# Sums of weight blocks: VectorE subtractions replaced by adding transfers from memory to memory

## The chip, the cores and the metric

The kernel runs on one core of one Trainium2 chip. The metric is the time of one execution on the device in microseconds (us), lower is better. The engines are named as in the profile: PE is TensorE (matmuls), with PEld for its weight loads; DVE is VectorE; ACT is ScalarE; POOL is GpSimd; SP is SyncE, which here issues nearly all transfers. A trailing q (SPq, POOLq) means the engine's instruction queue.

## The reference

A decoder trunk of two layers on 1024 tokens of width 1024, all float32. Layer one mixes tokens with HGRN2, a gated linear recurrence of 8 heads; layer two with sliding-window attention. Each layer ends with a gated feed-forward part:

```python
def conv_ffn(h, w_in, conv_w, conv_b, w_out):
    u = h @ w_in                                   # (1024, 1024) @ (1024, 5632)
    u = causal depthwise convolution of width 3 over u, + conv_b
    a, b = jnp.split(u, 2, axis=-1)
    return (jax.nn.silu(a) * b) @ w_out            # (1024, 2816) @ (2816, 1024)
...
    for layer in range(DEPTH):
        mix = hgrn2_mixer(...) if layer < N_A_LAYERS else swa_sink_mixer(...)
        h = layer_norm(ALPHA * h + mix, ...)
        h = layer_norm(ALPHA * h + conv_ffn(h, ...), ...)
```

The change is about the last product, the down-projection by `w_out`, and about the HGRN2 mixer of layer one, during which its weights are prepared.

## The kernel before, in words

Every float32 matrix is split into a high and a low part, and a product is three TensorE matmuls (`mm3`, lines 169 to 171). TensorE's order is written out in the program: a small planner (`Order`, `od`) hands out pieces of slower work (the recurrence's steps) between the matmuls of the projections. In the HGRN2 stage SyncE's order is the program's too; the orders on VectorE, ScalarE and GpSimd are made by the scheduler when the kernel is built, from its own estimate of when each operand is ready, with the program's order as priority. `tc.issue_after(x)` keeps what is made inside it behind `x` on `x`'s engine.

**The down-projection.** `Down` computes it in Winograd's form of Strassen's method: the activations (as blocks A) and the weights (as blocks B) are cut into 2 x 2 blocks, and seven block products take the place of eight. Some products need sums of weight blocks. There are four, s1 = B12 - B11, s3 = B22 - B12, s2 = B22 - s1, s4 = B21 - s2, all in the DRAM tensor `bsd` (one for each layer). `Down.sum_b` (line 539) loads pieces of 128 x 512 from it, `operands` makes the differences of activation blocks, and `evacuate` (line 589) adds each finished product to the rows of `Y` that it belongs to, in each of four pairs of token blocks.

**Where the sums are made.** No weight sum depends on the activations, so all are made early, in the HGRN2 stage. This stage is cut into 60 slots: 4 for the first head, then 8 for each of 7 heads (four half projections for q and f, four blocks for i and g). `slot_begin` (line 988) and `slot_end` (line 1007) stand around each. A table fixes for each of 22 pieces in which slot its two rows of blocks are loaded into rows of `Y` (line 998), in which VectorE makes the four subtractions (line 1005) and in which the result is stored to `bsd` (line 993). The subtractions are queued in `pending`; `between`, called in the recurrence, places two or four of them behind an instruction of the recurrence, and `slot_end` places the rest.

**The recurrence.** `recur` runs one head behind the projections. Its steps go through levels; in `update` (line 844) VectorE multiplies `qp` (line 851) and GpSimd `kp` (line 853), and the score matmuls of the next level (line 175) read both. GpSimd also makes small norms (lines 943 and 944). Weights of the projections of the next head are loaded by `load` (line 139, on SyncE) into three buffers `raw`, and split by ScalarE (line 151) and VectorE (line 144).

Of the kernel before, what the change touches and what calls it, by code (L numbers as in the profile page):

```python
# [10 lines left out]
F32 = mybir.dt.float32  # L11
# [76 lines left out]
def trunk(ctx: ExitStack, tc: tile.TileContext, a: dict, out: bass.AP):  # L88
    nc = tc.nc
# [8 lines left out]
    drp = ctx.enter_context(tc.tile_pool(name="drp", bufs=1, space=bass.MemoryType.DRAM))  # L98
# [11 lines left out]
    ynd = drp.tile([P, 8, D], F32, name="ynd")  # L110
    gd = drp.tile([P, NF, S], F32, name="gd")
    rbd = drp.tile([16, P, 2 * P], F32, name="rbd")
    bsd = [drp.tile([P, FF // 256, 2, D], F32, name=f"bsd{l}") for l in range(2)]

    def psmm():
        return mmp.tile([P, 512], F32, name="psmm")
# [400 lines left out]
    class Down:  # L517
# [19 lines left out]
            nc.sync.dma_start(dst, self.w[f0:f0 + P, bc * 512:(bc + 1) * 512])  # L537

        def sum_b(self, dst, k, t):
            i, j = {1: (0, 0), 3: (0, 1), 4: (1, 0), 2: (1, 1)}[t]  # L540
            nc.sync.dma_start(dst, self.sums[:, k, i, j * 512:(j + 1) * 512])

        def operands(self, i, k):
            p = self.ORDER[i]
            R = self.R[:, :, k, :] if i > 1 else None
            x = self.raw[0].rearrange("p (b n) -> p b n", b=2)
            self.raw = self.raw[1:] + self.raw[:1]
            if p == 1:
                self.block_a(x[:, 0], k, 0, 0)
                self.block_b(x[:, 1], k, 0, 0)  # L550
            elif p == 2:
                self.block_a(x[:, 0], k, 0, 1)
                self.block_b(x[:, 1], k, 1, 0)
            elif p == 5:
                self.block_a(R[:, 0], k, 1, 0)
                self.block_a(x[:, 0], k, 1, 1)
                self.sum_b(R[:, 1], k, 1)
                tt(R[:, 0], R[:, 0], x[:, 0], op=add)
                x = R
            elif p == 6:  # L560
                self.block_a(x[:, 0], k, 0, 0)
                self.sum_b(R[:, 1], k, 2)
                tt(R[:, 0], R[:, 0], x[:, 0], op=sub)
                x = R
            elif p == 7:
                self.block_a(x[:, 0], k, 1, 1)
                self.sum_b(x[:, 1], k, 3)
                tt(x[:, 0], x[:, 0], R[:, 0], op=sub)
            elif p == 3:
                self.block_a(x[:, 0], k, 0, 1)  # L570
                self.block_b(x[:, 1], k, 1, 1)
                tt(x[:, 0], x[:, 0], R[:, 0], op=sub)
            else:
                self.block_a(x[:, 0], k, 1, 1)
                self.sum_b(x[:, 1], k, 4)
            slots = {3: [10, 11, 12, 13, 14, 2, 7, 8, 9, 0, 1], 4: [6, 3, 4, 5, 2, 0, 1, 6, 3, 4, 5]}
            j = slots[p][k] if p in slots and not self.last else (i * self.H + k) % 15
            j = (j + 4) % 7 if j < 7 else j
            if j < 6:
                hl = hl_at(j)  # L580
            elif j == 6:
                hl = tail["R"][:, :2, :]
            else:
                hl = T[:, (j - 7) // 4, (j - 7) % 4 * 2:(j - 7) % 4 * 2 + 2, :]
            hl = hl.rearrange("p h (b n) -> p h b n", b=2)
            split(hl[:, 0], hl[:, 1], x)
            return hl

        def evacuate(self, p, tb, ps, ln):
            lo, hi = [Y[:, t, :].rearrange("p (h n) -> p h n", h=2) for t in (tb, tb + 4)]  # L590
            both = ps.unsqueeze(1).to_broadcast([P, 2, 512])
            if p == 1:
                for y in (lo, hi):
                    nc.vector.scalar_tensor_tensor(y, y, ALPHA, both, op0=ALU.mult, op1=ALU.add)
            elif p in (6, 7):
                tt(hi, hi, both, op=add)
            for y in {2: [lo[:, 0]], 5: [lo[:, 1], hi[:, 1]], 6: [lo[:, 1]], 3: [lo[:, 1]], 4: [hi[:, 0]]}.get(p, []):
                tt(y, y, ps, op=add)

            if p in (2, 3, 4, 7):  # L600
                ln_half(tb if p in (2, 3) else tb + 4, 0 if p in (2, 4) else 1)
            if p in (3, 4):
                task = ln(tb if p == 3 else tb + 4, self)
                if task is not None:
                    self.tasks.append(od.spawn(task))
# [53 lines left out]
    x = a["x"][0]  # L659
# [3 lines left out]
    with tc.tile_pool(name="t", bufs=1, reuse_waits="tile") as raws, hgrn_pool as hp:  # L663
# [154 lines left out]
        def recur(h, qs, fg, kp):  # L818
# [25 lines left out]
            def update(i):  # L844
                m = 1 << i
                nb = S // (2 * m)
                Tm, off = level
                qv = qp.rearrange("p (b u m) -> p b u m", u=2, m=m)
                kv = kp.rearrange("p (b u m) -> p b u m", u=2, m=m)
                tv = Tm[:, off:off + 2 * nb].rearrange("p (b u) -> p b u", u=2)  # L850
                nc.vector.tensor_tensor(qv[:, :, 1, :], qv[:, :, 1, :],
                                        tv[:, :, 0:1].to_broadcast([P, nb, m]), op=ALU.mult)
                (nc.gpsimd if i else nc.vector).tensor_tensor(kv[:, :, 0, :], kv[:, :, 0, :],  # L853
                                        tv[:, :, 1:2].to_broadcast([P, nb, m]), op=ALU.mult)
                noff = 0 if i == 0 else off + 2 * nb
                last = nc.vector.tensor_tensor(tot[:, noff:noff + nb], tv[:, :, 0], tv[:, :, 1], op=ALU.mult)
                level[:] = tot, noff
                return last

            yield 0.0  # L860
            r0 = hp.tile([P, S], F32, name="St")
# [23 lines left out]
            for i in range(2, 7):  # L885
# [3 lines left out]
                else:  # L889
# [9 lines left out]
                    def put():  # L899
                        for b in range(P // (2 * m)):  # L900
                            o = 2 * m * b
                            nc.scalar.copy(A[o:o + m, :, o + m:o + 2 * m], pv[o:o + m, :, o + m:o + 2 * m])
                last = update(i)
                between(put() or last, 2)
                if i == 4:
                    for b in range(P // BL):
                        bs = slice(b * BL, (b + 1) * BL)
# [35 lines left out]
            nc.gpsimd.tensor_scalar(ss, ss, 1.0 / P, RMS_EPS, op0=ALU.mult, op1=ALU.add)  # L943
            nc.gpsimd.tensor_tensor(ss, ss, nhalf.to_broadcast([P, NB]), op=ALU.pow)
            nc.vector.tensor_tensor(og, pv, G, op=ALU.mult)
            between(nc.vector.tensor_tensor(og, og, ss.unsqueeze(2).to_broadcast([P, NB, P]), op=ALU.mult), 4)
            values_done[0] = h
            yield 8.0
            ps = psax()
# [10 lines left out]

        pairs = FF // 256
        lead = [0, 3, 2, 2, 2, 2, 1, 1]
        begins = [4] + [8 * h + lead[h] for h in range(1, NH)]
        busy = {s for c in begins for s in (c - 1, c)}
        free, loads, sums, stores = {r: 0 for r in (0, 2, 4, 6)}, {}, {}, {}
        for i in range(2 * pairs):
            for s in range(8 * NH):
                for r in free:  # L970
                    at = next(n for n in range(s + 2, 9 * NH) if n not in busy and n not in sums)
                    if s not in loads and free[r] <= s and at + 1 <= begins[r] + 4:
                        break
                else:
                    continue
                break
            loads[s], sums[at], stores[at + 1], free[r] = (i, r), (i, r), (i, r), at + 2
        slot_no = [-1]
        anchor, pending = {}, []

        def between(inst, n):

            with tc.issue_after(inst.ins):
                while pending and n:
                    pending.pop(0)()
                    n -= 1

        def slot_begin():
            slot_no[0] += 1
            n = slot_no[0]  # L990
            if n in stores:
                i, r = stores[n]
                nc.sync.dma_start(bsd[i // pairs][:, i % pairs, :, :], Y[:, r:r + 2, :])
            if n in loads:
                i, r = loads[n]
                for k in range(2):
                    row = (k * pairs + i % pairs) * P
                    nc.sync.dma_start(Y[:, r + k, :], a["ffn_w_out"][i // pairs][row:row + P, :])
            if n in sums:
                r = sums[n][1]  # L1000
                blocks = Y[:, r:r + 2, :].rearrange("p a (b n) -> p a b n", b=2)
                (b11, b12), (b21, b22) = [(blocks[:, k, 0], blocks[:, k, 1]) for k in range(2)]

                for x, y, z in ((b11, b12, b11), (b12, b22, b12), (b22, b22, b11), (b21, b21, b22)):
                    pending.append(lambda x=x, y=y, z=z: tt(x, y, z, op=sub))

        def slot_end(act, dve, *makes):
            anchor["act"], anchor["dve"] = act, dve or anchor.get("dve", act)
            with tc.issue_after(anchor["act"].ins), tc.issue_after(anchor["dve"].ins):
                for make in makes:  # L1010
                    make()
                while pending:
                    pending.pop(0)()

        values_done = [-1]
        wo = a["hgrn_w_out"][0]
# [393 lines left out]
```

## Time and profile before

| | |
|---|---|
| times of three runs | 2218.33, 2218.30, 2216.71 us, median 2218.3 |
| the profiled execution, span from first to last instruction | 2212.6 us |
| mean granted TensorE clock | 0.998 |
| busy: PE, DVE, ACT, POOL | 2177.4, 1787.0, 931.6, 177.7 us |
| moved by DMA | 281.16 MB, mean 127 GB/s |

For the profiled execution the profile gives the span alone; what lies around it (launch and end) is seen only as the distance to the times of the runs. In a row of the profile, `out<-in` are tiles of the program, `x88` is the number of instructions, and "idle before" is the time in which the engine stood still just before them, with what ended it. A matmul's recorded end is modelled, and successive matmuls overlap in the records.

### The profile page before, as it was taken

What the parts mean: (1) busy time and instruction counts of PE and PEld (TensorE: products, weight loads), DVE (VectorE), ACT (ScalarE), POOL (GpSimd) and SP (SyncE); (2) the same over time, 40 slices, a digit from 0 to 9 for tenths busy, and PEclk for the clock granted to TensorE, in tenths of its full rate; (3) what the DMA queues carried; (4) which work ended last, traced back from release to release, by engine and by line L of the source; (5) the groups of instructions that cost most, each with busy time, mean ns of one, the idle gap of its engine ahead of it and who ended that gap; (6) DMA issues with size and microseconds to landing.
All of it is one profiled execution on the core that took longest, in us unless ns stands there. A gap on an engine that the chain in (4) does not pass through costs nothing.

```text
span 2212.6 us, 33398 instructions
## 1 busy us (share of the span) xinstructions
PE 2177.4 (98%) x13135; PEld 1812.6 (82%) x13135; DVE 1787.0 (81%) x2415; ACT 931.6 (42%) x1601; POOL 177.7 (8%) x196
## 2 busy tenths in 40 slices
PE   8999999999999999999999999999999999999998
PEld 7888888888888888887888887778888888887887
DVE  2777666566789888888997788887899888889987
ACT  4333333332844443344334446655554443343431
POOL 0121111210100000000000012211000000000001
PEclk9999999999999999999999999999999999999999
DMA  5555443252222222238854431114123222249663
GB/s 196 191 191 172 153 172 116 69 125 86 87 85 86 84 78 86 86 96 272 279 171 130 115 89 34 34 63 138 67 96 96 78 75 85 86 144 318 202 215 134
DMA packets 231943, 281.16 MB, mean 127 GB/s; under 512 B 29977, under 2 KB 160746, under 8 KB 228970
## 3 DMA queue, kind: packets, MB, share of 16 engines
q1 hardware_dynamic: 228736, 276.53, 38.5%
q10 hardware_dynamic: 3050, 2.49, 0.9%
q8 instruction: 103, 1.69, 0.3%
q14 instruction: 54, 0.44, 0.1%
HBM read 213.96 MB, written 65.01 MB: 126 GB/s over the span
## 4 chain that ended last, share of the span: by engine, by line
PE 82%; DVE 9%; DMA 3%; ACT 3%; issue 2%; POOL 1%; SPq 0%; ACTq 0%; DVEq 0%; POOLq 0%
PE psmm L169 17%; PE psmm L171 16%; PE psmm L170 16%; PE psax L171 8%; PE psax L169 8%; PE psax L170 8%; PE psax L175 3%; DVE T L144 1%; PE psmm L175 1%; DMA rx<-in_ffn_w_in_dram 1%; DVE HL L144 1%; PE psax L179 1%; ACT Y L244 1%; PE psax L1200 1%; PE psax L1203 1%
## 5 line engine op out<-in xcount | busy, mean ns | idle before, releaser
L169 PE MATMUL psmm<-T,HL 128*128 128x512 f32 x768 | 308.1, 401 | 0.0
L170 PE MATMUL psmm<-T,HL 128*128 128x512 f32 x768 | 300.7, 392 | 3.8 <-DVE T L144 2.1
L171 PE MATMUL psmm<-T,HL 128*128 128x512 f32 x768 | 301.3, 392 | 0.0
L474 DVE SCALAR_TENSOR_TENSOR Y<-Y,cwt 128x1023 f32<-128x1023 f32 (+1 forms) x176 | 225.3, 1280 | 40.1 <-ACT Y L472 39.9
L472 ACT ACTIVATE Y<-Y,cwt 128x1024 f32<-128x1024 f32 x88 | 109.1, 1240 | 263.6 <-DVE Y L461 260.0
L169 PE MATMUL psmm<-HL,T 128*128 128x256 f32 (+1 forms) x656 | 199.6, 304 | 1.5 <-ACT T L196 1.5
L171 PE MATMUL psmm<-HL,T 128*128 128x256 f32 (+1 forms) x656 | 195.4, 298 | 1.6 <-DVE T L144 1.6
L170 PE MATMUL psmm<-HL,T 128*128 128x256 f32 (+1 forms) x656 | 195.1, 297 | 1.2 <-DVE HL L144 1.2
L196 ACT CAST HL<-rx 128x1024 fp32r<-128x1024 f32 (+1 forms) x137 | 140.3, 1045 | 122.6 <-DMA rx<-in_ffn_w_in_dram 33.3
L144 DVE TENSOR_TENSOR HL<-rx,HL 128x1024 fp32r<-128x1024 f32 (+1 forms) x137 | 165.9, 1213 | 14.9 <-ACT HL L196 14.3
L171 PEld LDWEIGHTS psmm<-T,HL 128*128 128x128 f32 x768 | 144.6, 188 | 33.5 <-issue 1.9
L170 PEld LDWEIGHTS psmm<-T,HL 128*128 128x128 f32 x768 | 144.7, 188 | 31.3 <-DVE T L144 2.9
L169 PEld LDWEIGHTS psmm<-T,HL 128*128 128x128 f32 x768 | 144.6, 188 | 31.3 <-issue 1.4
L171 PE MATMUL psax<-T,HL 128*128 128x512 f32 x352 | 137.6, 391 | 0.0
L169 PE MATMUL psax<-T,HL 128*128 128x512 f32 x352 | 137.5, 391 | 0.0
L170 PE MATMUL psax<-T,HL 128*128 128x512 f32 x352 | 137.4, 390 | 0.0
L169 PEld LDWEIGHTS psmm<-HL,T 128*128 128x128 f32 x656 | 126.2, 192 | 8.1 <-issue 2.5
L171 PEld LDWEIGHTS psmm<-HL,T 128*128 128x128 f32 x656 | 126.0, 192 | 5.7 <-DVE T L144 2.5
L170 PEld LDWEIGHTS psmm<-HL,T 128*128 128x128 f32 x656 | 126.2, 192 | 4.9 <-DVE HL L144 1.7
L218 POOL TENSOR_TENSOR rs<-rs,nhalf 128x1 f32<-128x1 f32 x32 | 26.0, 813 | 1291.4 <-DVE rs L217 1291.1
L853 POOL TENSOR_TENSOR kp<-kp,tot 128x512 f32<-128x512 f32 x48 | 72.9, 1519 | 290.0 <-PE psax L175 149.3
L144 DVE TENSOR_TENSOR HL<-raw,HL 128x1024 fp32r<-128x1024 f32 x51 | 64.0, 1254 | 21.7 <-ACT HL L151 21.6
(295 smaller groups left out, 5257.9 us busy)
## 6 DMA issues: line engine op xcount, KB each, us to landing
rx<-in_ffn_w_in_dram SPq DMA_DIRECT2D x136, 256.0 KB, 3.4
rx<-gd SPq DMA_DIRECT2D x118, 256.0 KB, 3.7
Y<-in_ffn_w_out_dram SPq DMA_DIRECT2D x44, 512.0 KB, 6.0
bsd<-Y SPq DMA_DIRECT2D x22, 1024.0 KB, 4.8
gd<-Y SPq DMA_DIRECT2D x44, 512.0 KB, 2.7
rx<-in_ffn_w_out_dram SPq DMA_DIRECT2D x54, 256.0 KB, 4.0
R<-bsd SPq DMA_DIRECT2D x44, 256.0 KB, 4.3
Y<-in_ffn_w_in_dram SPq DMA_DIRECT2D x40, 256.0 KB, 3.3
```

Of the source, the lines that this page charges most:

```text
L144: make = lambda e: e.tensor_tensor(lo, src, hi.bitcast(F32), op=ALU.subtract)
L169: nc.tensor.matmul(ps, st(0), mv(0), start=start, stop=False)
L170: nc.tensor.matmul(ps, st(0), mv(1), start=False, stop=False)
L171: nc.tensor.matmul(ps, st(1), mv(0), start=False, stop=stop)
L175: nc.tensor.matmul(ps, lhsT, rhs, start=start, stop=stop, **kw)
L179: nc.tensor.transpose(ps, src, ident)
L196: nc.scalar.copy(hi, src)
L218: nc.gpsimd.tensor_tensor(rs, rs, nhalf, op=ALU.pow)
L244: nc.scalar.activation(hf[:, kc, :], ps[:, k * P:(k + 1) * P], AF.Identity, bias=shift, scale=scale)
L472: nc.scalar.activation(c, u, AF.Identity, bias=cwt[:, l, 3, ci:ci + 1], scale=cwt[:, l, 2, ci:ci + 1])
L474: nc.vector.scalar_tensor_tensor(c[:, sh:], u[:, :S - sh], cwt[:, l, 2 - sh, ci:ci + 1], c[:, sh:], op0=ALU.mult, op1=ALU.add)
L853: (nc.gpsimd if i else nc.vector).tensor_tensor(kv[:, :, 0, :], kv[:, :, 0, :], tv[:, :, 1:2].to_broadcast([P, nb, m]), op=ALU.mult)
```

## The change

The sums are no longer made on VectorE. Each layer's four sums become four DRAM tensors of 1408 x 512, in which 8 parts in all (2 layers, 4 parts of 352 rows) are filled by transfers from memory to memory: SyncE copies a block (`nc.sync.dma_start`), and a transfer issued from GpSimd with `accum_op=add` adds another block to it. Since a transfer can only add, all sums are now sums without a minus: s1 = B12 + B11, s3 = B12 + B22, s2 = s1 + B22, s4 = s2 + B21. The operand differences and the evacuations get other signs to fit. A part takes six slots in six stages, and a new part starts every seven slots: copies of stage 0, 2 and 4 are issued at a slot's beginning, additions of stage 1, 3 and 5 at a slot's end. `between` and its calls in `recur` go.

```diff
-    bsd = [drp.tile([P, FF // 256, 2, D], F32, name=f"bsd{l}") for l in range(2)]
+    bsd = [[drp.tile([FF // 2, D // 2], F32, name=f"bs{l}{t}") for t in range(4)] for l in range(2)]
...
-            i, j = {1: (0, 0), 3: (0, 1), 4: (1, 0), 2: (1, 1)}[t]
-            nc.sync.dma_start(dst, self.sums[:, k, i, j * 512:(j + 1) * 512])
+            nc.sync.dma_start(dst, self.sums[t - 1][k * P:(k + 1) * P, :])
...
-                tt(R[:, 0], R[:, 0], x[:, 0], op=add)
+                tt(R[:, 0], x[:, 0], R[:, 0], op=sub)
...
+            left, right = [Y[:, tb::4, h * 512:(h + 1) * 512] for h in range(2)]
             lo, hi = [Y[:, t, :].rearrange("p (h n) -> p h n", h=2) for t in (tb, tb + 4)]
             both = ps.unsqueeze(1).to_broadcast([P, 2, 512])
             if p == 1:
-                for y in (lo, hi):
-                    nc.vector.scalar_tensor_tensor(y, y, ALPHA, both, op0=ALU.mult, op1=ALU.add)
-            elif p in (6, 7):
-                tt(hi, hi, both, op=add)
-            for y in {2: [lo[:, 0]], 5: [lo[:, 1], hi[:, 1]], 6: [lo[:, 1]], 3: [lo[:, 1]], 4: [hi[:, 0]]}.get(p, []):
-                tt(y, y, ps, op=add)
+                for y, op in ((left, add), (right, sub)):
+                    nc.vector.scalar_tensor_tensor(y, y, ALPHA, both, op0=ALU.mult, op1=op)
+            elif p == 5:
+                tt(right, right, both, op=sub)
+            elif p == 6:
+                tt(right, right, both, op=add)
+                tt(hi[:, 0], hi[:, 0], ps, op=sub)
+            elif p == 7:
+                tt(hi[:, 0], hi[:, 0], ps, op=add)
+                tt(hi[:, 1], hi[:, 1], ps, op=sub)
+            else:
+                y, op = {2: (lo[:, 0], add), 3: (lo[:, 1], sub), 4: (hi[:, 0], add)}[p]
+                tt(y, y, ps, op=op)
...
-                last = update(i)
-                between(put() or last, 2)
+                update(i)
+                put()
...
+        NCH, RCH = 4, FF // 8
+        plan = {}
+        for i in range(2 * NCH):
+            for stage in range(6):
+                plan.setdefault(2 + 7 * i + stage, []).append((i // NCH, i % NCH, stage))
+        slot_no, anchor = [-1], {}
+
+        def sum_step(l, c, stage):
+
+            b1, b2, b3, b4 = [bsd[l][t][c * RCH:(c + 1) * RCH, :] for t in range(4)]
+            blk = lambda i, j: a["ffn_w_out"][l][i * FF // 2 + c * RCH:i * FF // 2 + (c + 1) * RCH,
+                                                 j * D // 2:(j + 1) * D // 2]
+            copies = {0: ((b1, blk(0, 1)), (b3, blk(0, 1))), 2: ((b2, b1),), 4: ((b4, b2),)}
+            sums = {1: ((b1, blk(0, 0)), (b3, blk(1, 1))), 3: ((b2, blk(1, 1)),), 5: ((b4, blk(1, 0)),)}
+            for dst, src in copies.get(stage, ()):
+                nc.sync.dma_start(dst, src)
+            for dst, src in sums.get(stage, ()):
+                nc.gpsimd.dma_start(dst, src, accum_op=ALU.add)
 
         def slot_begin():
             slot_no[0] += 1
-            n = slot_no[0]
...
+            for step in plan.get(slot_no[0], ()):
+                if step[2] % 2 == 0:
+                    sum_step(*step)
 
         def slot_end(act, dve, *makes):
             anchor["act"], anchor["dve"] = act, dve or anchor.get("dve", act)
             with tc.issue_after(anchor["act"].ins), tc.issue_after(anchor["dve"].ins):
+                for step in plan.get(slot_no[0], ()):
+                    if step[2] % 2:
+                        sum_step(*step)
                 for make in makes:
                     make()
-                while pending:
-                    pending.pop(0)()
```

More of the change, by code (lines that the diff above doesn't have):

```diff
@@ L562, in operands @@
                 self.sum_b(R[:, 1], k, 2)
-                tt(R[:, 0], R[:, 0], x[:, 0], op=sub)
+                tt(R[:, 0], R[:, 0], x[:, 0], op=add)
                 x = R
@@ L567, in operands @@
                 self.sum_b(x[:, 1], k, 3)
-                tt(x[:, 0], x[:, 0], R[:, 0], op=sub)
+                tt(x[:, 0], R[:, 0], x[:, 0], op=sub)
             elif p == 3:
@@ L571, in operands @@
                 self.block_b(x[:, 1], k, 1, 1)
-                tt(x[:, 0], x[:, 0], R[:, 0], op=sub)
+                tt(x[:, 0], R[:, 0], x[:, 0], op=sub)
             else:
@@ L855, in update @@
                 noff = 0 if i == 0 else off + 2 * nb
-                last = nc.vector.tensor_tensor(tot[:, noff:noff + nb], tv[:, :, 0], tv[:, :, 1], op=ALU.mult)
+                nc.vector.tensor_tensor(tot[:, noff:noff + nb], tv[:, :, 0], tv[:, :, 1], op=ALU.mult)
                 level[:] = tot, noff
-                return last
             yield 0.0
@@ L945, in recur @@
             nc.vector.tensor_tensor(og, pv, G, op=ALU.mult)
-            between(nc.vector.tensor_tensor(og, og, ss.unsqueeze(2).to_broadcast([P, NB, P]), op=ALU.mult), 4)
+            nc.vector.tensor_tensor(og, og, ss.unsqueeze(2).to_broadcast([P, NB, P]), op=ALU.mult)
             values_done[0] = h
@@ L957, in recur @@
                     split_scaled(T[:, 0, h, ts], T[:, 1, h, ts], ps[:, ts], par[:, 80:81])
-        pairs = FF // 256
         lead = [0, 3, 2, 2, 2, 2, 1, 1]
[L965 to L984, printed above, removed]
-                    pending.pop(0)()
-                    n -= 1
+        NCH, RCH = 4, FF // 8
[14 more added lines that the diff above has]
+                nc.gpsimd.dma_start(dst, src, accum_op=ALU.add)
@@ L988, in slot_begin @@
         def slot_begin():
             slot_no[0] += 1
-            n = slot_no[0]
[L991 to L1005, printed above, removed]
+            for step in plan.get(slot_no[0], ()):
+                if step[2] % 2 == 0:
+                    sum_step(*step)
@@ L1009, in slot_end @@
             with tc.issue_after(anchor["act"].ins), tc.issue_after(anchor["dve"].ins):
+                for step in plan.get(slot_no[0], ()):
+                    if step[2] % 2:
+                        sum_step(*step)
                 for make in makes:
                     make()
-                while pending:
-                    pending.pop(0)()
         values_done = [-1]
```

## The prediction

> **What bounds the kernel now.** I read the page first (busy shares and chain), then the busy time in stretches of 100 us, then who TensorE waited for in the stage that the change touches, then the rows of the pieces themselves.
>
> ```profile
> span 2212.6 us, 33398 instructions
> PE 2177.4 (98%) x13135; PEld 1812.6 (82%) x13135; DVE 1787.0 (81%) x2415; ACT 931.6 (42%) x1601; POOL 177.7 (8%) x196
> PE 82%; DVE 9%; DMA 3%; ACT 3%; issue 2%; POOL 1%; SPq 0%; ACTq 0%; DVEq 0%; POOLq 0%
> ```
>
> TensorE is busy 98% of the span and carries 82% of the chain; VectorE is the only other engine with a share there that counts. The sums of weight blocks run in the first mixer (HGRN2), at 55.6 to 417.4 us by their row further down. In the stretches there (PE, PEld, DVE, ACT, POOL, clock, DMA share, GB/s) it reads:
>
> ```profile
> 100.00:200.00 100.00, 99.69 (x1166) 88.77 (x1166) 73.98 (x118) 30.88 (x81) 21.49 (x16) 1.00 0.58 199
> 200.00:300.00 100.00, 100.00 (x1011) 90.88 (x1010) 67.89 (x108) 32.48 (x79) 15.51 (x12) 1.00 0.49 168
> 300.00:400.00 100.00, 98.31 (x1044) 86.78 (x1043) 63.14 (x97) 34.19 (x84) 18.90 (x16) 1.00 0.33 111
> 400.00:500.00 100.00, 95.87 (x1109) 83.72 (x1108) 57.17 (x84) 35.08 (x71) 19.49 (x14) 0.98 0.45 107
> ```
>
> TensorE has 0.3 + 0 + 1.7 + 4.1 = 6.1 us of idle time in these 400 us, while VectorE is busy 57 to 74% and GpSimd under 22%. TensorE's waits from 50 to 520 us (total, times, longest) are:
>
> ```profile
> PE psmm L780 <- DVE og L945: 2.0, 1, 2.0
> PE psmm L170 <- issue: 1.7, 1, 1.7
> PE psax L175 <- DVE qp L851: 1.4, 3, 0.5
> PE psmm L170 <- DVE HL L144: 1.2, 2, 0.6
> PE psax L175 <- DVE og L869: 0.9, 1, 0.9
> ```
>
> So the stage is bound by TensorE, whose order is written out by hand and is not changed. Work taken off VectorE can be worth only what is left in that list; anything that makes TensorE late costs in full.
>
> **The change part by part.** *VectorE's 88 subtractions go.* Their rows, by form and by source line (there: shortest, median, longest in ns, first and last start):
>
> ```profile
> L1005 DVE TENSOR_TENSOR Y<-Y 128x512 f32<-128x512 f32 x88 | 70.0, 796 | 4.2 <-DMA Y<-in_ffn_w_out_dram 3.0
> L1005 DVE TENSOR_TENSOR Y<-Y x88: 675/692/1605, 55.6 to 417.4; 128x512 f32<-128x512 f32 x88
> ```
>
> That is 70.0 us of VectorE. On the path lie only the waits for the recurrence's operands, L851 with 1.4 and L869 with 0.9 us: a gain of 2.3, of which I take 2. The wait at L780 lies in one place, after an activation chain; L144's are splits that remain. The bounds of this gain are 0 and the 6.1 us of all idle time, of which 4.1 lie after 400 us, where the subtractions end at 417.4.
>
> *SyncE's transfers change.* Out go 44 loads of 512 KB and 22 stores of 1 MB; in come 32 copies from memory to memory of 352 rows x 2 KB = 704 KB (8 parts, 4 copies each). Rows: KB, then median us from issue to landing; then the issue times and what SyncE waited for.
>
> ```profile
> Y<-in_ffn_w_out_dram SPq DMA_DIRECT2D x44, 512.0 KB, 6.0
> bsd<-Y SPq DMA_DIRECT2D x22, 1024.0 KB, 4.8
> L993 SPq DMA_DIRECT2D bsd<-Y x22: 326/338/4132, 59.5 to 419.0; - x22
> SPq L993 <- DVE Y L1005: 240.6, 18, 40.0
> SPq L998 <- DMA bsd<-Y: 40.3, 13, 4.5
> ```
>
> Issuing is about 0.34 us each, so 66 x 0.34 = 22 us against 32 x 0.34 = 11 us on a queue that is mostly waiting: nothing on the path. By the load's pace (6.0 us for 512 KB) a copy of 704 KB lands after 8.3 us, by the store's (4.8 us for 1 MB) after 3.3 us. What matters is the waiting in order: the copy of block sum 1 into 2 waits until the addition into 1 has landed, that of 2 into 4 until the addition into 2 has, and the loads of the next head's projection weights are queued behind them. Before, the same queue stood 240.6 us for VectorE's sums, 13.4 us each and 40.0 at most. How much the weights bear is seen where SyncE issues them and where ScalarE first uses them:
>
> ```profile
> 227.25 6.06 SPq L139 DMA_DIRECT2D raw<-in_hgrn_w_in_dram  x4
> 257.61 3.74 SPq L139 DMA_DIRECT2D raw<-in_hgrn_w_in_dram  x2
> 258.64 1.04 ACT L151 CAST HL<-raw 128x1024 fp32r<-128x1024 f32 x1
> 287.88 1.05 ACT L151 CAST HL<-raw 128x1024 fp32r<-128x1024 f32 x1
> raw<-in_hgrn_w_in_dram SPq DMA_DIRECT2D x16, 512.0 KB, 8.3
> ```
>
> The group issued by 233.3 has landed by 241.6 at 8.3 us and is used at 258.6: 17 us of cover. The next, issued by 261.4 and landed by 269.7, is used at 287.9: 18 us. I cost SyncE's new waits at nothing, hidden by these 17 us; if that cover is gone, every further microsecond is TensorE's (the second rival).
>
> *GpSimd issues 32 adding transfers of 704 KB.* No DMA on GpSimd is in the trace. Its issue I bound by SyncE's 0.34 us below and its longest, 4.1 us, above; I take 1.5 us, GpSimd's ordinary instruction. Each also waits, in GpSimd's order, until the copy that it adds to has landed. Queued behind it are the recurrence's updates (kp, L853) and the small norms (L943, L944). The updates of one head, the first of the next, and the score matmuls that wait for them:
>
> ```profile
> 182.89 1.61 POOL L853 TENSOR_TENSOR kp<-kp,tot 128x512 f32<-128x512 f32 x1 [9.42 <-PE psax L175]
> 186.29 1.11 POOL L853 TENSOR_TENSOR kp<-kp,tot 128x512 f32<-128x512 f32 x1 [1.79 <-PE psax L175]
> 189.93 1.52 POOL L853 TENSOR_TENSOR kp<-kp,tot 128x512 f32<-128x512 f32 x1 [2.54 <-PE psax L175]
> ...
> 197.49 1.49 POOL L853 TENSOR_TENSOR kp<-kp,tot 128x512 f32<-128x512 f32 x1 [2.39 <-PE psax L175]
> ...
> 240.72 1.60 POOL L853 TENSOR_TENSOR kp<-kp,tot 128x512 f32<-128x512 f32 x1 [12.04 <-PE psax L175]
> 185.38 0.76 PE L175 MATMUL psax<-qp,kp 128*32 128x32 f32 x64
> 189.02 0.76 PE L175 MATMUL psax<-qp,kp 128*32 128x32 f32 x64
> 192.67 0.70 PE L175 MATMUL psax<-qp,kp 128*32 128x32 f32 x32
> ```
>
> An update ends at 184.50, 187.40, 191.45 and is used at 185.38, 189.02, 192.67: slack 0.9, 1.6, 1.2, mean 1.2 us. The updates come every 3.6 us from 182.89 to 198.98, 16.1 us of a head's 57.8 (182.89 to 240.72): 28% of the time. Eight slots a head make a slot 7.2 us. A hold of w us in the series delays an update by w - 1.8 on average (half the pitch), and TensorE by w - 1.8 - 1.2. With the issue alone, w = 1.5, that is nothing. The additions come in 8 x 3 = 24 groups, so 24 x 28% = 6.7 meet the series. For the hold, 0 is the lower end (the addition is placed a slot behind its copy and finds it landed). The upper one is 10 us: a copy at the load's pace, 8.3 us, and 1.5 of issue. I take 5 us, near the longest wait that SyncE had for a landing (4.5 us). Then 6.7 x (5 - 3.0) = 13.4, with those that begin just ahead of the series 14 us. With 10 us it is 24 x (28% + 9%) = 8.9 meetings of 7 us, 62 us.
>
> The Trainium skill's page "DMA: Bandwidth & Descriptors" (Anatomy of one DMA) fits a GpSimd-issued transfer as about 2.0 us plus its bytes at 436 GB/s. For 704 KB that makes an estimated 3.7 us; the trace's 512 KB load, 6.0 us where the fit gives 3.2, does not agree. With copies so quick the hold would shrink to some 2 us and the sum to a gain of 2: the first rival.
>
> *The signs of the seven products.* Rows of the evacuations before:
>
> ```profile
> L596 DVE TENSOR_TENSOR Y<-Y,psax 128x1024 f32<-128x1024 f32 x4 | 4.9, 1216 | 0.0
> L598 DVE TENSOR_TENSOR Y<-Y,psax 128x512 f32<-128x512 f32 x12 | 8.0, 683 | 1.1 <-PE psax L171 1.1
> ```
>
> Product 5 has one instruction of 1024 columns in place of two of 512 (2 x 683 - 1216 = 150 ns saved, 4 token blocks, 2 layers), product 7 the reverse: nil. The operand differences swap inputs in place: nil. Reading the sums back takes the same 256 KB a piece, off TensorE's path: nil.
>
> The sum: 2212.6 - 2 + 14 = 2224.6 us of span. The runs' median, 2218.3, lies 5.7 us above the profiled span, launch and end outside the instructions; with it 2230.
>
> **The rivals.** *Nothing is held.* The additions find their copies landed and GpSimd, idle 78% and more, hides the issue; what is left is the gain: 2216, and at best, with all idle time of the stage gone, 2218.3 - 6.1 = 2212.2. For it: the 1.2 us of slack and the slot between copy and addition. Against: GpSimd's order is set when the kernel is built, and there a transfer is only a guess of its landing. To be faster by over 0.2% (4.4 us, about what a measurement of this kernel can tell from no change) it needs most of the 6.1 us, though the waits named for VectorE's operands are 2.3: little chance.
>
> *SyncE's order paces the stage.* One chain per part: copies 1 and 3, both additions, copy 2, its addition, copy 4, and only then the next part, which comes every 7 slots, 50.6 us. With copies of 8.3 us and additions of twice that (they read the target too), SyncE is held 8.3 + 16.6 + 8.3 + 16.6 = 50 us where each pair runs side by side, and 16.6 + 33.2 + 8.3 + 16.6 = 75 us where it runs one behind the other. The surplus over 50.6 is paid in each of 8 parts: nothing at 50, 93 us halfway (62), 195 at 75. It decides from an addition of 8.6 us (pairs one behind the other: 24.9 + 3 x 8.6 = 50.6) to one of 17 us (side by side: 16.6 + 2 x 17). For it: SyncE's order is fixed, and L998 already waits for a landing 13 times. Against: at the store's pace, 3.3 us a copy and 6.6 an addition, the chain is 20 to 33 us, and the weights have 17 us of cover.
>
> The Trainium skill, on the page "DMA: Bandwidth & Descriptors" (Two DMAs through the same engine are not ordered), wants the issuing engine to wait for the first transfer's semaphore before a dependent one; by it both holds are real waits of SyncE and GpSimd. The trace agrees: SyncE's L998 waits for the landing of bsd, 40.3 us in 13 times.
>
> **How the numbers follow.** Held updates, 48%: 2223 to 2280, likeliest 2230. Nothing held, 35%: 2212 to 2222, of this 10% below 2213.9. SyncE paces, 17%: from 2223 up, most of it over 2280 (2311 halfway). Faster by over 0.2% is 0.10, within 0.2% is 0.25, slower 0.65. The range goes from 2212 (all idle time gone) to 2280 (holds of 10 us) and leaves out some 15 in 100.
>
> **What would show it.** Right: no L1005 on VectorE (70 us less); in GpSimd's waits, adding transfers that wait for a copy, several us each; TensorE's list from 50 to 520 us gains waits on POOL kp L853 of 10 to 20 us in all, and the stage ends that much later. The first rival: no such waits. The second: TensorE or ScalarE wait for DMA raw<-in_hgrn_w_in, and SyncE's longest waits are for additions over 14 us. I would be wrong altogether if time moved after 520 us, where only signs change.

## The result, and the profile after

The changed kernel is slower by 6%: 2349.76 us median (2345.98 to 2355.46, 4 runs) against 2218.32 (2216.71 to 2220.05, 4 runs) on the same chip, a ratio of 1.0597 with a 95% interval of 1.0583 to 1.0611. The forecast was 2230 us in a range of 2212 to 2280: the sign is right, the size is out by more than a factor of ten (131 us more instead of 12).

The page of the changed kernel: span; busy time by engine; TensorE's granted clock in 40 slices of 59 us; the chain by engine.

```profile
span 2351.2 us, 33300 instructions
PE 2210.4 (94%) x13135; PEld 1840.7 (78%) x13135; DVE 1713.4 (73%) x2327; ACT 930.0 (40%) x1601; POOL 206.3 (9%) x228
PEclk9897988989999999999999999999999999999999
PE 73%; DMA 8%; DVE 7%; issue 5%; ACT 3%; POOL 2%; SPq 0%; ACTq 0%; DVEq 0%; POOLq 0%
```

VectorE lost 73.6 us (1787.0 to 1713.4), and the span grew by 138.6 us all the same (the runs' medians differ by 131: the profiled executions are single ones). Of the 138.6, TensorE's idle time is 105.6 (2351.2 - 2210.4 = 140.8, against 35.2 before), and 33.0 are the same 13135 matmuls taking longer (2177.4 to 2210.4). The clock row says where: it has digits under 9 in the first nine slices only (a digit is the clock in tenths).

Busy time in stretches (us, PE, PEld, DVE, ACT, POOL, clock, DMA share, GB/s), the mixer first, then one stretch of the up-projection:

```profile
100.00:200.00 100.00, 86.14 (x824) 78.07 (x825) 42.14 (x73) 26.27 (x70) 21.93 (x19) 0.89 0.48 107
200.00:300.00 100.00, 76.72 (x812) 68.79 (x810) 33.55 (x57) 22.38 (x53) 17.21 (x15) 0.88 0.52 120
300.00:400.00 100.00, 71.80 (x774) 63.11 (x775) 29.20 (x50) 19.81 (x48) 20.45 (x17) 0.86 0.51 107
400.00:500.00 100.00, 86.02 (x812) 75.08 (x811) 36.05 (x65) 29.42 (x73) 18.27 (x15) 0.90 0.45 109
...
900.00:1000.00 100.00, 100.00 (x438) 81.81 (x437) 88.43 (x101) 42.38 (x50) 0.00 (x0) 1.00 0.25 79
```

Where 1011 to 1166 matmuls ran in 100 us before, 774 to 824 run now, with TensorE idle 14 to 28% and its clock at 0.86 to 0.90. From the up-projection on nothing is changed (438 matmuls in the last row, 437 in the same 100 us before). Who TensorE waited for up to 700 us (total, times, longest):

```profile
PE psax L175 <- POOL kp L860: 74.2, 10, 16.3
PE psax L179 <- DVE og L952: 26.9, 4, 9.5
...
PE psax L179 <- POOL kp L860: 4.3, 1, 4.3
```

These 15 waits sum to 105.4 us, which is all of the new idle time (105.6). Eleven are for GpSimd's update of kp (L860; L853 before). Four are for og on VectorE (L952), which takes its factor from the norms that GpSimd works out in ss (L949 and L950; L943 and L944 before). No weight load of the recurrence is in this list. What GpSimd itself waited for at the additions (L987):

```profile
POOL bs L987 <- DMA bs<-bs: 130.8, 12, 25.7
POOL bs L987 <- issue: 109.0, 14, 10.5
...
POOL bs L987 <- DMA bs<-in_ffn_w_out_dram: 72.6, 6, 21.7
```

GpSimd stood still ahead of each of the 32 additions, 312.4 us in all and 9.8 us on average; such a stand is called a hold. Two kinds are to be told apart: 18 holds (203.4 us) end with the landing of the copy that is added to, and 14 (109.0 us) have no releaser in the trace ("issue"). One head's stretch of GpSimd's timeline, with TensorE's matmul that waited (start, us, engine, line, idle before):

```profile
211.95 1.05 POOL L987 DMA_DIRECT2D bs<-in_ffn_w_out_dram  x1 [11.45 <-DMA bs<-bs]
220.84 0.95 POOL L987 DMA_DIRECT2D bs<-in_ffn_w_out_dram  x1 [7.85 <-issue]
228.22 0.94 POOL L987 DMA_DIRECT2D bs<-in_ffn_w_out_dram  x1 [6.43 <-issue]
228.84 1.50 POOL L860 TENSOR_TENSOR kp<-kp,tot 128x512 f32<-128x512 f32 x1
230.39 1.08 PE L175 MATMUL psax<-qp,kp 128*32 128x32 f32 x64 [16.26 <-POOL kp L860]
```

Three additions stand in GpSimd's order directly ahead of the update. The second is issued 7.9 us after the first has been, the third 6.4 us after the second; only then may the update run, and TensorE has lost 16.26 us. Additions issue in 0.95 us and land a median of 7.7 us later (issues of the transfers: KB, us to landing):

```profile
bs<-in_ffn_w_out_dram POOLq DMA_DIRECT2D x32, 704.0 KB, 7.7
...
bs<-in_ffn_w_out_dram SPq DMA_DIRECT2D x16, 704.0 KB, 7.8
bs<-bs SPq DMA_DIRECT2D x16, 704.0 KB, 5.7
```

So the second addition starts about when the first has landed, and the third when the second has: as if GpSimd had room for one such transfer at a time. The other kind of hold is seen a head later, in the timeline of SyncE and GpSimd together:

```profile
209.01 41.50 SPq L139 DMA_DIRECT2D raw<-in_hgrn_w_in_dram  x2
250.56 0.58 SPq L985 DMA_DIRECT2D bs<-bs  x1
256.91 0.96 POOL L987 DMA_DIRECT2D bs<-in_ffn_w_out_dram  x1 [10.93 <-DMA bs<-bs]
```

GpSimd stands from 245.98 for a copy that SyncE issues only at 250.56, because the copy is behind two loads of projection weights, the second of which is issued at 250.1; the copy then lands after some 6 us. The loads themselves wait until VectorE has split the weights loaded before (L144). SyncE's longest waits, up to 700 us, are these, 365.6 us where the kernel before has 56.8:

```profile
SPq L139 <- DVE HL L144: 365.6, 18, 40.7
```

The instructions of the copies and of the additions, by source line (shortest, median, longest in ns, first and last start):

```profile
L985 SPq DMA_DIRECT2D bs<-in_ffn_w_out_dram x16: 505/603/2038, 22.6 to 490.8; - x16
L985 SPq DMA_DIRECT2D bs<-bs x16: 474/481/582, 59.0 to 545.2; - x16
```

```profile
L987 POOL DMA_DIRECT2D bs<-in_ffn_w_out_dram x32: 932/954/1213, 31.5 to 550.4; - x32
```

With the start of each of these 32 and 32 from the timelines, 100 of the 203 us in the 18 holds pass before the copy is issued. In about 25 of these the copy itself waits for the addition issued just before (four holds); in 75, SyncE is still at something else. The remaining 104 us are copies in flight.

### The profile page after: what moved, and what is told of

It reads as the page before. It is cut to its first block, busy times and chain, and to the rows that moved or that the text cites. A ratio compares the mean times of both kernels' runs of the same rounds, so it can differ in the third digit from the quotient of the medians.

```text
span 2351.2 us, 33300 instructions
## 1 busy us (share of the span) xinstructions
PE 2210.4 (94%) x13135; PEld 1840.7 (78%) x13135; DVE 1713.4 (73%) x2327; ACT 930.0 (40%) x1601; POOL 206.3 (9%) x228
## 4 chain that ended last, share of the span: by engine, by line
PE 73%; DMA 8%; DVE 7%; issue 5%; ACT 3%; POOL 2%; SPq 0%; ACTq 0%; DVEq 0%; POOLq 0%
PE psmm L169 14%; PE psmm L171 14%; PE psmm L170 14%; PE psax L171 8%; PE psax L170 8%; PE psax L169 8%; DMA bs<-in_ffn_w_out_dram 4%; DMA bs<-bs 2%; PE psax L175 2%; DVE HL L144 1%; PE psmm L175 1%; PE psax L179 1%; DVE T L144 1%; ACT Y L244 1%; PE psax L1189 1%
## 5 line engine op out<-in xcount | busy, mean ns | idle before, releaser
L169 PE MATMUL psmm<-T,HL 128*128 128x512 f32 x768 | 314.0, 409 | 0.0
L170 PE MATMUL psmm<-T,HL 128*128 128x512 f32 x768 | 305.4, 398 | 2.1 <-DVE T L144 2.1
L171 PE MATMUL psmm<-T,HL 128*128 128x512 f32 x768 | 305.7, 398 | 0.0
L472 ACT ACTIVATE Y<-Y,cwt 128x1024 f32<-128x1024 f32 x88 | 109.0, 1238 | 264.2 <-DVE Y L461 260.6
L169 PE MATMUL psmm<-HL,T 128*128 128x256 f32 (+1 forms) x656 | 204.5, 312 | 1.8 <-ACT T L196 1.8
L171 PE MATMUL psmm<-HL,T 128*128 128x256 f32 (+1 forms) x656 | 199.3, 304 | 2.1 <-DVE T L144 2.1
L170 PE MATMUL psmm<-HL,T 128*128 128x256 f32 (+1 forms) x656 | 199.3, 304 | 1.2 <-DVE HL L144 1.2
L144 DVE TENSOR_TENSOR HL<-rx,HL 128x1024 fp32r<-128x1024 f32 (+1 forms) x137 | 165.7, 1212 | 15.9 <-ACT HL L196 15.4
L169 PEld LDWEIGHTS psmm<-T,HL 128*128 128x128 f32 x768 | 148.0, 193 | 32.6 <-issue 1.4
L170 PEld LDWEIGHTS psmm<-T,HL 128*128 128x128 f32 x768 | 148.2, 193 | 32.2 <-DVE T L144 2.9
L171 PEld LDWEIGHTS psmm<-T,HL 128*128 128x128 f32 x768 | 147.3, 192 | 32.7
L858 DVE TENSOR_TENSOR qp<-qp,tot 128x512 f32<-128x512 f32 x48 | 36.7, 765 | 147.1 <-PE psax L175 146.8
L169 PEld LDWEIGHTS psmm<-HL,T 128*128 128x128 f32 x656 | 131.1, 200 | 8.5 <-issue 2.5
L171 PEld LDWEIGHTS psmm<-HL,T 128*128 128x128 f32 x656 | 130.4, 199 | 6.2 <-DVE T L144 3.1
L170 PEld LDWEIGHTS psmm<-HL,T 128*128 128x128 f32 x656 | 130.8, 199 | 5.0 <-DVE HL L144 1.7
L175 PE MATMUL psax<-qp,kp 128*32 128x32 f32 (+1 forms) x2048 | 35.7, 212 | 75.2 <-POOL kp L860 74.2
```

The lines of the kernel that those rows point to most:

```text
L144: make = lambda e: e.tensor_tensor(lo, src, hi.bitcast(F32), op=ALU.subtract)
L169: nc.tensor.matmul(ps, st(0), mv(0), start=start, stop=False)
L170: nc.tensor.matmul(ps, st(0), mv(1), start=False, stop=False)
L171: nc.tensor.matmul(ps, st(1), mv(0), start=False, stop=stop)
L175: nc.tensor.matmul(ps, lhsT, rhs, start=start, stop=stop, **kw)
L472: nc.scalar.activation(c, u, AF.Identity, bias=cwt[:, l, 3, ci:ci + 1], scale=cwt[:, l, 2, ci:ci + 1])
```

## The experiments

Three causes could do this. The first (A) is GpSimd's order: holds at the additions make the updates and norms behind them late. The rivals are SyncE's order (B), by which copies and weight loads wait for each other and pace the stage, and the traffic from memory to memory itself (C), slowing whatever else is loaded. Ratios are against the kernel before, on the same chip, with 95% intervals; its medians there were 2217.4 to 2218.1 us.

**The additions left out.**

```diff
-                nc.gpsimd.dma_start(dst, src, accum_op=ALU.add)
+                pass
```

> The kernel after without its 32 adding transfers, so the sums lack their second terms; the 32 copies stay on SyncE. Theory A: nothing is left on GpSimd that waits, so 2214 to 2219 us, the gain of 2 us for the 88 subtractions included. Theory C, traffic of the copies: over 2230. Theory B: between, since copies of copies still wait for landings on SyncE, but not over 2225.

Measured: 2213.1 us (10 runs), ratio 0.9984 (0.9974 to 0.9993). All that is lost comes in with the additions, so the copies' traffic alone (C) is not the cause; B is not told from A here, since without additions no copy waits for one. What is left is the gain of the rest of the change, VectorE's relief in the main: 0.16%, 3.5 us (1.6 to 5.8 by the interval), where the prediction took 2.

**The signs alone**, with the sums on VectorE as before:

```diff
-                tt(R[:, 0], R[:, 0], x[:, 0], op=add)
+                tt(R[:, 0], x[:, 0], R[:, 0], op=sub)
...
+                for y, op in ((left, add), (right, sub)):
+                    nc.vector.scalar_tensor_tensor(y, y, ALPHA, both, op0=ALU.mult, op1=op)
```

> The kernel before with the new signs alone: VectorE makes the sums as before, with add in place of sub, and operands and evacuations are those of the kernel after. All theories here: 2216 to 2221 us, no difference. If the evacuations' strided pairs of rows cost something, it shows here as over 2223.

Measured: 2217.33 us (10 runs), ratio 0.9995 (0.9986 to 1.0004): nil, as predicted and expected.

**Nothing urgent on GpSimd.** All transfers stay where the change put them; the updates and norms leave GpSimd's queue.

```diff
-                (nc.gpsimd if i else nc.vector).tensor_tensor(kv[:, :, 0, :], kv[:, :, 0, :],
+                nc.vector.tensor_tensor(kv[:, :, 0, :], kv[:, :, 0, :],
...
-            nc.gpsimd.tensor_scalar(ss, ss, 1.0 / P, RMS_EPS, op0=ALU.mult, op1=ALU.add)
-            nc.gpsimd.tensor_tensor(ss, ss, nhalf.to_broadcast([P, NB]), op=ALU.pow)
+            nc.vector.tensor_scalar(ss, ss, 1.0 / P, RMS_EPS, op0=ALU.mult, op1=ALU.add)
+            nc.vector.tensor_tensor(ss, ss, nhalf.to_broadcast([P, NB]), op=ALU.mult)
```

> The kernel after with the kp updates and both instructions of the small norms on VectorE (the power of the norms is left out: a multiplication of the same size stands in its place). All 64 transfers stay as they are, descriptors' memory 1024. Theory A (GpSimd's order): nothing that TensorE needs is behind a transfer any more; GpSimd still waits some 400 us for landings and room, TensorE's waits for og go (33.4 us in the kernel with kp alone on VectorE), and the time is 2212 to 2222 us. Theory B (SyncE's order) or C (memory): TensorE keeps losing time to late weights or slow transfers, 2230 or more.

Measured: 2218.83 us (10 runs), ratio 1.0001 (0.9992 to 1.0010), as A expected. GpSimd's waits at the additions in this kernel are:

```profile
POOL bs L987 <- DMA bs<-bs: 149.4, 11, 25.4
...
POOL bs L987 <- issue: 127.4, 15, 10.6
POOL bs L987 <- DMA bs<-in_ffn_w_out_dram: 116.9, 6, 26.8
```

This run decides. GpSimd stands longer than in the changed kernel, 393.7 us, the same 64 transfers move the same bytes, and it costs nothing, since nothing that TensorE needs stands behind: no wait for og behind the norms, and 0.8 us for kp, is left in TensorE's list. Neither SyncE's order nor the traffic by itself is the cause of the 131 us.

**Only the updates moved** (the first hunk of the edit above, the norms left on GpSimd):

```diff
-                (nc.gpsimd if i else nc.vector).tensor_tensor(kv[:, :, 0, :], kv[:, :, 0, :],
+                nc.vector.tensor_tensor(kv[:, :, 0, :], kv[:, :, 0, :],
```

> The kernel after, with the recurrence's kp updates of levels 1 to 6 on VectorE; the small norms stay on GpSimd. Theory A: TensorE's 78.5 us of waits for kp vanish, the 26.9 us for og behind the norms stay, and with the clock recovering in part the time is 2235 to 2260 us. Theory B (SyncE's order, late weights) and theory C (the transfers slow the memory for all): 2340 to 2355, because no transfer moves.

Measured: 2263.0 us (4 runs), ratio 1.0209 (1.0188 to 1.0229), 3 us over the range that A expected. The updates account for 87 of the 131 us. What is left is the norms' part, in TensorE's waits:

```profile
PE psax L179 <- DVE og L952: 33.4, 4, 16.8
```

TensorE's new idle time here is 34.0 us (span 2259.6 less 2190.4 busy, less 35.2). The prediction had named the norms as queued behind the additions, but gave them no term.

**Room for descriptors.** In the kernel, `dynamic_dma_scratch_size` is the memory kept for the descriptors of GpSimd's transfers.

```diff
-    nc = bacc.Bacc("TRN2", target_bir_lowering=False, num_devices=1, dynamic_dma_scratch_size=1024)
+    nc = bacc.Bacc("TRN2", target_bir_lowering=False, num_devices=1, dynamic_dma_scratch_size=4096)
```

> The kernel after, with dynamic_dma_scratch_size 4096 in place of 1024 (the memory in which GpSimd keeps its transfers' descriptors). Theory A, GpSimd's order: TensorE waits for updates that stand behind adding transfers in GpSimd's queue. Of GpSimd's waits before these transfers, 109.0 us in 14 cases have no cause in the profile and follow another adding transfer by 7 to 10 us. If they are waits for room for descriptors, they vanish here, the rest (203.4 us for landings) stays, and the time falls to 2290 to 2320 us. If they are something else: 2350. Theory B, SyncE's order paces the stage: 2350 too, since its copies still wait for the additions.

Measured: 2299.59 us (4 runs), ratio 1.0371 (1.0352 to 1.0390), 50 us less than the changed kernel and within what A expected. GpSimd's waits at the additions:

```profile
POOL bs L987 <- DMA bs<-bs: 183.1, 16, 31.4
...
POOL bs L987 <- DMA bs<-in_ffn_w_out_dram: 83.9, 16, 21.6
```

The 109 us without a releaser are gone: they were room for descriptors. The holds for landings stay, 267.0 us against 203.4, as the queue reaches the next landing sooner. TensorE's waits fall from 105.4 to 69.4:

```profile
PE psax L175 <- POOL kp L860: 47.7, 10, 11.1
PE psax L179 <- DVE og L952: 13.5, 3, 6.3
PE psax L179 <- POOL kp L860: 8.2, 1, 8.2
```

**Additions placed by hand.** The first two additions of a part, and the last one of the part before, are put behind the last update of a head, the remaining one behind an early update of the next head, and the copies at fixed steps of `recur`, so that GpSimd stands for them while nothing urgent is behind.

```diff
+            with tc.issue_after(update(1).ins):
+                sum_step(h - 1, 3)
...
+                k_inst = update(i)
+                if i == 4:
+                    sum_step(h - 1, 4)
+                if i == 6:
+                    with tc.issue_after(k_inst.ins):
+                        sum_step(h, 1)
+                        sum_step(h - 1, 5)
```

> The kernel after with the additions placed in GpSimd's order by hand, descriptors' memory 1024: those of blocks 1 and 3 of a part and of block 4 of the part before behind a head's last kp update, that of block 2 behind the first kp update of the next head; copies in the recurrence's steps, well ahead. Theory A: no addition finds its copy missing in front of a kp; but three additions in a row take about 8 us each with room for one, so the norms that come 15 us after the last update are held by 3 to 10 us in most heads, of which 1 to 5 reach TensorE: 2220 to 2250 us.

Measured: 2256.7 us (4 runs), ratio 1.0166 (1.0149 to 1.0183), 7 us over what was expected. In GpSimd's waits the holds without a releaser remain, two for each of the eight parts, and TensorE waits 28.0 us for og behind the norms:

```profile
POOL bs L996 <- issue: 133.8, 16, 11.1
```

The same placement with 4096 bytes for descriptors:

> As the kernel with the additions placed by hand, with descriptors' memory 4096. Theory A: three additions in a row take 3 us, done before the norms; 2212 to 2219 us, as the kernel without additions, and so as fast as the kernel before or 1 to 5 us faster. If additions as such slow the core (memory, descriptors written beside VectorE), over 2222.

Measured: 2239.84 us (5 runs), ratio 1.0091 (1.0078 to 1.0105): 17 us less, but not the 2212 to 2219 that A expected. Here GpSimd issues three additions one after the other (its timeline):

```profile
145.94 2.89 POOL L996 DMA_DIRECT2D bs<-in_ffn_w_out_dram  x3
```

Busy time by stretch, this kernel, columns as above:

```profile
100.00:400.00 300.00, 299.70 (x3231) 268.24 (x3230) 151.96 (x255) 97.37 (x244) 77.77 (x64) 1.00 0.61 143
400.00:650.00 250.00, 222.97 (x1690) 188.38 (x1689) 141.56 (x222) 98.64 (x202) 37.04 (x40) 0.95 0.52 128
```

and the same stretches of the kernel before:

```profile
100.00:400.00 300.00, 298.00 (x3216) 266.43 (x3216) 205.02 (x322) 97.54 (x244) 55.91 (x43) 1.00 0.47 159
400.00:650.00 250.00, 244.75 (x1812) 206.31 (x1811) 168.67 (x253) 113.07 (x218) 30.04 (x32) 0.99 0.33 92
```

For 300 us the placed additions cost nothing: 15 matmuls more than before in the same time. So in this stretch the additions as such do not slow the core, which was the other case of the expectation. The loss is after 400 us, where the last head's additions have no further head to stand behind. There GpSimd stands 13.89 and 12.11 us for two landings directly ahead of the last norm:

```profile
520.50 0.93 POOL L996 DMA_DIRECT2D bs<-in_ffn_w_out_dram  x1 [13.89 <-DMA bs<-bs]
533.53 0.92 POOL L996 DMA_DIRECT2D bs<-in_ffn_w_out_dram  x1 [12.11 <-DMA bs<-bs]
534.53 0.20 POOL L958 TENSOR_SCALAR ss<-ss 128x8 f32<-128x8 f32 x1
```

and TensorE waits for what comes out of it:

```profile
PE psax L179 <- DVE og L961: 11.9, 1, 11.9
```

This is 11.9 of the 19.8 us of new idle time. Two other waits, 7.4 us for qp on VectorE (L858) and 5.7 us for a load of convolution weights (L787), were not traced to their cause.

So the last head's steps were moved into the first up-projection, issued from GpSimd, copies and all:

```diff
+            with tc.issue_after(last_norm[0].ins):
+                for i, stage in [(6, 3), (7, 0), (6, 4), (7, 1), (6, 5), (7, 2), (7, 3), (7, 4), (7, 5)] if self.l == 0 else []:
+                    sum_step(i, stage, nc.gpsimd)
```

> As the kernel with the additions placed by hand and descriptors' memory 4096, with the steps that fell into the last head's recurrence moved to GpSimd's idle time in the first up-projection. In the kernel placed by hand TensorE lost 11.9 us behind a norm held by two additions of the last head, and 7.4 and 5.7 us near it. Theory A: these go, 2212 to 2220 us. If the other 6 heads' placed additions cost something of their own, it stays at 2230 or more.

Measured: 2231.92 us (5 runs), ratio 1.0067 (1.0055 to 1.0080), again over the 2212 to 2220 that A expected. The waits of that head for og and qp are gone, the one for the convolution weights stays (5.8 us), and a new one of 9.7 us stands at the beginning of the up-projection (all engines' waits from 600 to 700 us):

```profile
PE psmm L169 <- DVE Y L472: 9.7, 1, 9.7
DVE rx L441 <- DMA rx<-in_ffn_w_in_dram: 9.1, 1, 9.1
```

VectorE is late because weights of the up-projection are late. Their landing from 600 to 660 us, in this kernel and in the kernel before:

```profile
rx<-in_ffn_w_in_dram SPq DMA_DIRECT2D x8, 256.0 KB, 19.6
```

```profile
rx<-in_ffn_w_in_dram SPq DMA_DIRECT2D x10, 256.0 KB, 4.0
```

This is the traffic's price, 19.6 us a load against 4.0, and it is the third cause after all. In the kernel placed by hand with 4096 bytes, which has no such transfers at this point, the loads land after 4.3 us. In the changed kernel's mixer it cost nothing that the times show (the run with nothing urgent on GpSimd); here TensorE has no cover. The Trainium skill says on the page "DMA: Bandwidth & Descriptors" (Issuing engines are not separate DMA queues) that transfers started from different engines run on the same 16 DMA engines and interleave; the two rows agree.

**All steps in the up-projections**, behind the last norm before each, on GpSimd, with 1024 bytes for descriptors:

```diff
+            with tc.issue_after(last_norm[0].ins):
+                for i, stage in [(4 * self.l + c, s) for s in range(6) for c in range(4)]:
+                    sum_step(i, stage, nc.gpsimd)
```

> The kernel after with all sums moved out of the HGRN2 stage: the 32 transfers of each layer's sums (16 copies and 16 additions) are all issued from GpSimd behind its last norm ahead of that layer's up-projection, where GpSimd has nothing else to do; descriptors' memory 1024, so with room for one transfer of about 8 us, 256 us of the 400 that the stage lasts. Theory A (GpSimd's order): the waits are as many as before and cost nothing, since nothing that TensorE needs stands behind them: 2211 to 2217 us, at or a little under the kernel before. If transfers from memory to memory slow the weight loads of the up-projection: 2220 or more, with TensorE waiting behind DMA rx<-in_ffn_w_in.

Measured: 2225.65 us (5 runs), ratio 1.0046 (1.0032 to 1.0060). This is over the 2211 to 2217 that A expected, and in the range of the other case, slowed weight loads. The mixer is free, 3231 matmuls from 100 to 400 us. The loss has moved to where the sums now are:

```profile
650.00:1050.00 400.00, 393.23 (x1700) 319.64 (x1699) 352.44 (x388) 163.04 (x184) 15.32 (x20) 1.00 0.54 148
1600.00:2000.00 400.00, 395.63 (x1712) 322.03 (x1711) 352.02 (x395) 166.51 (x190) 19.09 (x24) 1.00 0.53 137
```

Before, the same stretches held 1733 and 1742 matmuls, and DMA was busy 35 and 31% instead of 54 and 53%. TensorE's waits there are few, mostly for splits on VectorE and ScalarE, and 2.6 us at the longest; none is for a load itself. From 600 to 660 us the weights land after

```profile
rx<-in_ffn_w_in_dram SPq DMA_DIRECT2D x10, 256.0 KB, 7.7
```

instead of 4.0 us. That late weights make the splits late is likely by this row; no run separates it from other causes.

None of these placements beats the kernel before. With the additions left out altogether the gain is 0.16%, so a placement that hid them wholly could be expected to earn that and no more.

## Why the prediction was wrong in size

**Right:** the mechanism (additions held in GpSimd's order, updates behind them late, TensorE late in full), its place (nothing moves from the up-projection on), the signs (nil), VectorE's relief (3.5 us measured, 2 taken), and SyncE's new waits: the 17 us of cover for the weights held in the mixer. The issue was put at 1.5 us and took 0.95. Of the 5.7 us added for launch and end, a run shows 1.8 (2353.0 us, span 2351.2); this matters little.

**Wrong: the hold, w = 5 us.** This is the term that failed most. It measured 9.8 us on average for an addition and up to 25.7; for each of the sum's 24 groups, with the issues, it is 14.3 us ((312.4 + 32 x 0.95) / 24). I thought of it as a landing, 0 to 10 us. The copies' median landings were within the bounds (5.7 and 7.8 us; the bounds were 3.3 and 8.3). The Trainium skill's page "DMA: Bandwidth & Descriptors" (Anatomy of one DMA), by whose fit an addition was an estimated 3.7 us, does not agree with the 7.7 us measured. (The load of 512 KB that the prediction held against this fit was issued from SyncE, so it could not test it.) But a hold begins when GpSimd comes to the addition and ends when SyncE has come to the copy and the copy has landed, and half of the time in the 18 holds that end with a landing (100 of 203 us) passed before the copy was issued. I had costed SyncE's lateness for the weights alone, though the row of L993, issued up to 40.0 us late, was in front of me: the change takes away the sums for which SyncE stood there, but SyncE then stands at the weight loads ahead of the copies. It does so when TensorE is not late, too: 242.9 us for VectorE's splits in the kernel with nothing urgent on GpSimd. And a third of all holds, 109 us, was room for descriptors: the sum had no term for it at all, although 24 groups of 32 additions put two in a row where a part has a pair.

**Wrong: the meetings, 6.7 of 24.** They measured 15, eleven with updates and four with norms, and each cost 7.0 us (105.4 / 15) where the sum took 5 - 3.0 = 2.0. I had spread the additions evenly over the head. In the timeline, 15 updates and norms start within 1.1 us of an addition's issue, so they had been standing right behind it. An addition that waits in order collects what follows: the longer the hold, the less chance is left that nothing urgent has come due. With w = 10 the sum gave 62 us as its upper bound. With the 14.3 us measured, its first term alone, 6.7 x (14.3 - 3.0), is an estimated 76 us in place of 13.4. By the sum's own formula, then, the size of the hold accounts for some 60 of the 91 us of waits that it lacked; how the rest divides between the groups that begin just ahead of the series, the norms, and the uneven spread stays open.

**Not foreseen: the clock.** The new waits explain 105 us; 33 more come from slower matmuls. Across three kernels, new idle time and added busy time go together: 105.6 and 33.0 us (the change), 69.4 and 20.6 (room for 4096 bytes), 34.0 and 13.0 (updates on VectorE). A microsecond of waiting cost TensorE about 1.3 to 1.4.

The rival "SyncE's order paces the stage" did not occur: it was to decide from an addition of 8.6 us, and additions landed in 7.7; TensorE never waits for projection weights, and the kernel with nothing urgent on GpSimd is as fast as before. Its place is taken by a mixture that neither case had: SyncE's order makes up a part of GpSimd's holds (75 of 312 us, outside its waits for additions), and GpSimd's order sets what they cost.

**Left open:** the split of the holds into lateness and landing is read from the timelines and was not varied by a run of its own. Why matmuls slow down with the waits was not varied either. The late load of convolution weights in the placed kernels, and the late splits with all steps in the up-projections, are not explained.

## What to carry to other kernels

A transfer that waits, on an engine that also computes, is a wait put into that engine's instruction stream: its price is not the mean idle time of the engine but what stands behind it in order, and the test is to move that work elsewhere and leave the transfers. A hold for another engine's transfer lasts until that engine has come to issue it, so its bound is the longest stretch that the issuer stands and a landing, not a landing alone. Before moving 70 us off an engine, look at what the bound engine waits for from it: here it was 2 us, and with the additions left out the gain was 0.16%.

## What the runs showed of the hardware

GpSimd has room for one adding transfer of 704 KB with 1024 bytes for descriptors (the next is issued about when the last has landed, after 6.2 to 10.5 us of hold in the changed kernel) and for at least three with 4096 (issued within 2.9 us). Until there is room GpSimd's own instructions stand, and the trace names no releaser.

TensorE's granted clock fell to 0.86 to 0.90 in stretches in which it was idle 14 to 28%, with single waits up to 16.3 us, and was at 1.00 from 600 us on, where these waits have ended. The Trainium skill's page "TensorE: Matmul & The Clock Gate" (HAM oscillation — how this bites in real kernels) has the rule that TensorE should have no idle gaps over some 3.4 us; the trace agrees in kind, since the 15 waits are 7.0 us long on average and the clock is full where there are none.
